# An S5 layer with GLU and ConvFFN: odd input tiles turned on TensorE, scanned states by GpSimd's queue, low halves of the GLU weights on VectorE

## The chip, the cores and the metric

One core of one Trainium2 chip runs the whole program. The metric is the device time of one execution in microseconds (us). The engines are called TensorE (PE), VectorE (DVE), ScalarE (ACT), GpSimd (POOL) and SyncE (SP); SyncE computes nothing here and only issues transfers. Each engine works through its own instructions in order; a transfer (DMA) is issued on the queue of one engine, SP, ACT or POOL.

## The reference

One layer with 2048 frames of 1024 channels, behind 16 learned meta tokens that are dropped at the end:

```python
h = jnp.concatenate([meta, x], axis=1)
hn = rms_norm(h, norm_mix[layer])
y = s5_mixer(hn, ...)           # below
h = h + y
hn = rms_norm(h, norm_ffn[layer])
h = h + conv_ffn(hn, ...)       # (silu(a) * b) @ w_down, a and b from a causal 3-tap conv of hn @ w_up
return h[:, N_META:]
```

The mixer is a linear recurrence with complex diagonal states in 64 groups of 16 channels, followed by a gated linear unit (GLU):

```python
u = (xn @ w_in).reshape(bsz, L, S5_GROUPS, S5_GROUP)
bu = einsum('gph,blgh->blgp', bb, u)              # complex input of the states
s = associative_scan(a * s_before + bu)           # 64 complex states a group
y = einsum(c_re, s_re) - einsum(c_im, s_im) + d_skip * u
y = gelu(y)
a, g = split(y @ w_glu, 2)
return a * sigmoid(g)
```

## The kernel before, in words

**Tiling.** Channels lie in eight blocks of 128 (`cb` or `p`, 0 to 7), frames in 16 tiles of 128, of which tile `r` takes every sixteenth frame; the meta tokens are a small 17th tile. Matrix products are made in f16 with three products: a value is held as a high half and a low half (`hi`, `lo`: the value minus its f16 rounding), and high × high, high × low and low × high are summed in fp32 (`mm3`, lines L76, L77, L78; in the GLU line L137).

**Head, to about 139 us.** For each x tile, `norm_a` (ACT squares, POOL makes 1/rms) and `norm_b` (L177 ACT high half, L178 DVE low half, L180 two transposing transfers on SP's queue, one for each half) put the normalised tile, turned so that channels are on the partitions, into `hnT`. The input weights come in column blocks; `split_win` scales them and makes their halves (ACT L354, L355, DVE L357 and others). `emit_u` makes u for a block and a quad of four tiles (512 columns), in parts as the tiles come; `evict_u` (POOL copies one column L404, ACT the rest L405) brings it from PSUM to `us`, and a transfer on SP to DRAM (`ud`), from where `load_u` fetches it as `U` in the order of the recurrence. Blocks 0, 1 and 2 are made in the head. In between `params` makes the recurrence's coefficients in small steps. An order written out by hand (a plan for each tile) sets what is emitted when.

**Periods p = 0 to 6, to about 408 us.** For block p: `gen_b`, `gen_c` on DVE (tables), `emit_v` on PE (the states' inputs), `scan(p)` on DVE (lines L547, L550, L552, in place in `S`), `emit_k` and `load_toep` (the Toeplitz matrix within 16 frames), `emit_z` (four transfers from the scanned `S` to `Z`, line L575), and one period later `emit_y(p-1)` on PE: products with Toep (L598, L599) and with Z (L600), gelu on ACT (L602) into `yf`, stored to `yd` by POOL (L606). PE fills up with the u of blocks 3 to 7 (`uq`). The last scan, p = 7, stands behind the loop.

**GLU weights.** `split_wg(i)` loads one of 16 slabs of 128 × 1024 on POOL's queue (L96) into a staging buffer `gst`, and makes its halves `wg`: a slab's high half by ACT in two steps (L102, L103) and its low half by POOL (L104), or both by DVE (L99, L100). Slab i belongs to depth `dk` = i // 2 of the product. Slabs 0 to 7 go by ACT and POOL in period 6 and beside the last scan, slabs 8 to 15 by DVE behind the last scan. `load_y` and `prep_y` fetch y from `yd` as `yt`, make its halves `yh` and turn them into `yT`; `glu_mm(t, d0, d1)` makes the products of tile t for depths d0 to d1.

**GLU loop (to about 739 us) and FFN.** 16 tiles of the GLU with the FFN's preparation, and then the FFN. The change does not touch them.

## Time and profile before

| | |
|---|---|
| median of 3 runs | 2039.63 us (2032.14 to 2040.07) |
| profiled execution | 2040.73 us, of which the span of the profile is 2038.9 us |
| granted TensorE clock, mean | 0.979 |
| busy over the span | PE 94%, DVE 68%, ACT 32%, POOL 28% |
| of this up to 739 us | the head, the scans and the GLU, where the change lies |

Rows of the profile are read like this: a group of instructions has its line, engine, operation, output <- inputs, the shape, the count, then busy time, mean ns of one, and the idle time in front of it with what ended it. A row of the timeline begins with start and length in us. A row by stage has the stretch, its length, the busy time of each engine with the count of instructions, the mean granted clock, the share of time for which the transfer engines were busy, and GB/s.

### The profile page before, as it was taken

Reading aid. Unit: us, or ns where it says so; the run is one execution under the profiler, and the core shown is the slowest. Engines: PE = TensorE matmul, PEld = TensorE weight load, DVE = VectorE, ACT = ScalarE, POOL = GpSimd, SP = SyncE. Lnnn points to the kernel's source line nnn. Section 1 sums busy time; section 2 is a strip of 40 time slices with the busy share of each in tenths; the row PEclk is TensorE's granted clock in tenths of the full one; section 3 lists DMA queues with packets and bytes.
Section 4 is the critical chain, followed back from the end, with each engine's and each line's share of the span. In section 5 each row is a group of like instructions: output and inputs, shape, how many; then the busy total and the mean of one; then the engine's idle time right before and its main releaser. Section 6 shows DMA issues by size and latency. Waiting matters only on the chain.

```text
span 2038.9 us, 28973 instructions
## 1 busy us (share of the span) xinstructions
PE 1923.3 (94%) x10992; PEld 957.5 (47%) x10992; DVE 1384.9 (68%) x1709; ACT 645.2 (32%) x1057; POOL 577.2 (28%) x644
## 2 busy tenths in 40 slices
PE   3699999689999999999999989999999999999999
PEld 3456666445444444444444434334444444444444
DVE  3489999944444348999999961345466666668982
ACT  5433423312222224544445441222222232322110
POOL 4221212400000014555555500366000001117630
PEclk9799999789999999999999999999999999999999
DMA  9967766958566656444444489999533333336443
GB/s 187 188 136 140 176 138 150 229 139 185 130 140 158 147 150 178 143 156 148 146 157 148 151 243 274 310 324 303 171 104 101 102 104 101 101 99 156 144 124 93
DMA packets 337223, 329.92 MB, mean 162 GB/s; under 512 B 150700, under 2 KB 238332, under 8 KB 337084
## 3 DMA queue, kind: packets, MB, share of 16 engines
q1 hardware_dynamic: 319164, 286.01, 52.9%
q0 software_dynamic: 8496, 27.30, 4.7%
q10 hardware_dynamic: 9424, 14.76, 2.9%
q8 instruction: 86, 1.41, 0.3%
q14 instruction: 53, 0.43, 0.1%
HBM read 183.82 MB, written 108.45 MB: 143 GB/s over the span
## 4 chain that ended last, share of the span: by engine, by line
PE 66%; DVE 8%; DMA 4%; issue 2%; ACT 1%; POOL 1%; SPq 1%; DVEq 0%; ACTq 0%; POOLq 0%
PE g L137 15%; PE p L78 11%; PE p L76 11%; PE p L77 11%; PE pq L76 3%; PE pq L77 3%; PE pq L78 3%; PE po L76 2%; PE po L77 2%; PE po L78 2%; DMA wc<-wcd 1%; DMA wcd<-wc 1%; DVE wc L914 1%; DVE y L1132 1%; DVE y L1131 1%
## 5 line engine op out<-in xcount | busy, mean ns | idle before, releaser
L76 PE MATMUL p<-hc,wc 128*128 128x512 f16 x1232 | 467.3, 379 | 2.3 <-DMA hc<-hl 1.7
L78 PE MATMUL p<-hc,wc 128*128 128x512 f16 x1232 | 467.5, 379 | 1.7 <-DVE wc L914 1.7
L77 PE MATMUL p<-hc,wc 128*128 128x512 f16 x1232 | 467.4, 379 | 0.9 <-DMA hc<-hl 0.9
L137 PE MATMUL g<-wg,yT 128*128 128x512 f16 x1536 | 334.3, 381 | 0.7 <-DMA yT<-yh 0.7
L914 DVE SCALAR_TENSOR_TENSOR wc<-fst,wc 128x512 f16<-128x512 f32 x209 | 184.7, 892 | 109.9 <-ACT wc L908 91.4
L137 PEld LDWEIGHTS <-yT 128*128 128x128 f16 x1536 | 150.2, 98 | 183.1 <-issue 2.6
L908 ACT ACTIVATE wc<-fst 128x512 f16<-128x512 f32 x209 | 125.9, 625 | 229.6 <-POOL fst L873 97.5
L78 PEld LDWEIGHTS <-wc 128*128 128x128 f16 x1232 | 120.2, 98 | 148.7 <-DVE wc L914 3.8
L76 PEld LDWEIGHTS <-wc 128*128 128x128 f16 x1232 | 120.1, 98 | 140.0 <-issue 1.8
L77 PEld LDWEIGHTS <-wc 128*128 128x128 f16 x1232 | 120.2, 98 | 138.9 <-DMA hc<-hl 1.2
L76 PE MATMUL pq<-wc,act 128*128 128x512 f16 x352 | 135.2, 384 | 16.6 <-DMA wc<-wcd 11.1
L76 PE MATMUL u<-hnT,win 128*128 128x512 f16 (+2 forms) x352 | 115.2, 337 | 25.6 <-DMA hnT<-hl 14.8
L77 PE MATMUL pq<-wc,act 128*128 128x512 f16 x352 | 135.1, 384 | 0.0
L78 PE MATMUL pq<-wc,act 128*128 128x512 f16 x352 | 134.8, 383 | 0.0
L77 PE MATMUL u<-hnT,win 128*128 128x512 f16 (+2 forms) x352 | 114.9, 337 | 16.9 <-DMA hnT<-hl 16.9
L76 PE MATMUL po<-wc,act 128*128 128x512 f16 x308 | 117.6, 382 | 3.4 <-DVE res L1292 3.4
L77 PE MATMUL po<-wc,act 128*128 128x512 f16 x308 | 117.6, 382 | 0.0
L78 PE MATMUL po<-wc,act 128*128 128x512 f16 x308 | 117.4, 381 | 0.0
L78 PE MATMUL u<-hnT,win 128*128 128x512 f16 (+2 forms) x352 | 115.0, 337 | 0.0
L1123 ACT ACTIVATE act<-hu,cwt 128x1024 f32<-128x1024 f32 x44 | 54.6, 1241 | 185.6 <-DVE hu L1224 141.3
L77 PEld LDWEIGHTS <-act 128*128 128x128 f16 x660 | 64.8, 98 | 99.1 <-issue 23.3
L1123 ACT ACTIVATE y<-hu,cwt 128x1024 f32<-128x1024 f32 x44 | 54.6, 1240 | 162.3 <-DVE hu L1224 123.2
(328 smaller groups left out, 2983.6 us busy)
## 6 DMA issues: line engine op xcount, KB each, us to landing
wc<-wcd SPq DMA_DIRECT2D x275, 256.0 KB, 2.7
wcd<-wc SPq DMA_DIRECT2D x253, 256.0 KB, 3.2
fst<-in_ffn_w_up_dram SPq DMA_DIRECT2D x44, 512.0 KB, 5.1
fst<-in_ffn_w_down_dram SPq DMA_DIRECT2D x44, 512.0 KB, 5.8
ud<-us SPq DMA_DIRECT2D x32, 258.0 KB, 5.3
U<-ud SPq DMA_DIRECT2D x16, 516.0 KB, 3.5
Toep<-kd SPq DMA_DIRECT2D x64, 128.0 KB, 5.4
yd<-yf POOLq DMA_DIRECT2D x8, 1024.0 KB, 7.6
```

Of the source, the lines that this page charges most:

```text
L76: PE.matmul(out=ps, lhsT=sh, rhs=mh, start=first, stop=False)
L77: PE.matmul(out=ps, lhsT=sh, rhs=ml, start=False, stop=False)
L78: PE.matmul(out=ps, lhsT=sl, rhs=mh, start=False, stop=last)
L137: PE.matmul(out=gps[t][o], lhsT=yT[t][:, a, dk], rhs=wg[b][:, dk, 512 * o:512 * o + 512], start=(dk == 0 and a + b == 0), stop=(dk == DK - ...
L908: A.activation(w[:, 0], src, AF.Copy, scale=GS)
L914: V.scalar_tensor_tensor(w[:, 1], src, GS, w[:, 0], op0=ALU.mult, op1=ALU.subtract)
L1123: A.activation(y, hu[:, 2:18], AF.Identity, bias=cwt[:, 3, c:c + 1], scale=cwt[:, 2, c:c + 1])
L1131: V.scalar_tensor_tensor(y, hu[:, 1:17], cwt[:, 1, c:c + 1], y, op0=ALU.mult, op1=ALU.add)
L1132: V.scalar_tensor_tensor(y, hu[:, 0:16], cwt[:, 0, c:c + 1], y, op0=ALU.mult, op1=ALU.add)
```

## The change

There are three parts.

*Head.* Odd tiles are no longer turned by transfers. `norm_t` scales the identity by 1/rms (DVE) and multiplies the x tile, in fp32, with it: eight products of 128 columns on PE, which turn and normalise at once; `norm_c` takes them out of PSUM as high half (ACT) and low half (DVE). Even tiles and the meta tile stay with `norm_b`. u is emitted by pairs of tiles (256 columns) for blocks 0, 1 and 2; the last quad of blocks 1 and 2 comes whole, behind that of block 0. The order is written anew: x loads six tiles ahead on ACT's queue, loads of the first tables in front of the transposes on SP, the split of the fourth weight block behind the last evictions; the small copy of `evict_u` moves from POOL to ACT.

*Queues.* `emit_z` issues on POOL's queue instead of SP's; the last block's `yd` store goes to SP; in period 6, `transp` and three slab loads are issued in front of Z.

*GLU weights.* ACT makes all 16 high halves, DVE all 16 low halves (by one subtraction from the scaled slab, L101), POOL none. There are nine staging slots. The first nine low halves stand directly behind the last scan, in front of what y's last block needs from DVE; products with high halves of depths 0 to 3 are emitted ahead of them, those with low halves behind them and in front of `emit_y(7)`; high halves 9 to 15 stand between and behind the gelus of `emit_y(7)`.

```diff
     def split_wg(i, pool, tag, bufs):
...
-        if wg_eng[0] is V:
-            V.tensor_scalar(wg[0][:, dk, cs_], st, GS, None, op0=ALU.mult)
-            V.scalar_tensor_tensor(wg[1][:, dk, cs_], st, GS, wg[0][:, dk, cs_], op0=ALU.mult, op1=ALU.subtract)
-        else:
-            A.activation(st, st, AF.Copy, scale=GS)
-            A.copy(wg[0][:, dk, cs_], st)
-            PO.tensor_tensor(wg[1][:, dk, cs_], st, wg[0][:, dk, cs_], op=ALU.subtract)
+        A.activation(st, st, AF.Copy, scale=GS)
+        A.copy(wg[0][:, dk, cs_], st)
+        yield
+        V.tensor_tensor(wg[1][:, dk, cs_], st, wg[0][:, dk, cs_], op=ALU.subtract)
+        yield
...
+        def norm_t(r, xt, rs):
+            dg = ld.tile([P, P], F32, tag="dg", bufs=1, name=f"dg{r}")
+            V.tensor_scalar(dg, ident, rs, None, op0=ALU.mult)
+            turned[r] = []
+            for h in range(2):
+                pt = psum.tile([P, 4, P], F32, tag="v", name=f"xT{r}_{h}")
+                for i in range(4):
+                    c = P * (4 * h + i)
+                    PE.matmul(out=pt[:, i], lhsT=xt[:, c:c + P], rhs=dg, start=True, stop=True)
+                turned[r].append(pt)
+
+        def norm_c(r):
+            for h, pt in enumerate(turned.pop(r)):
+                hi, lo = (t[:, 4 * h:4 * h + 4, r] for t in hnT)
+                A.copy(hi, pt)
+                V.tensor_tensor(lo, pt, hi, op=ALU.subtract)
...
-            PO.tensor_copy(us[:, :, 0:1], um[cb][:, 4 * q:4 * q + 4].unsqueeze(2))
+            A.copy(us[:, :, 0:1], um[cb][:, 4 * q:4 * q + 4].unsqueeze(2))
...
             for c in range(2):
                 for e in range(2):
-                    SY.dma_start(out=z.rearrange("p (q e) k -> p e q k", e=2)[64 * c:64 * c + 64, e],
+                    PO.dma_start(out=z.rearrange("p (q e) k -> p e q k", e=2)[64 * c:64 * c + 64, e],
                                  in_=S[cb][64 * e:64 * e + 64, :, c])
...
         for i, r in enumerate(seq):
...
+            if i + 2 < len(seq):
+                r2 = seq[i + 2]
+                (norm_t if r2 % 2 else norm_b)(r2, xt.pop(r2), na.pop(r2))
+            if i + 1 < len(seq) and seq[i + 1] in turned:
+                norm_c(seq[i + 1])
...
+            elif r % 2:
+                if r % 4 == 1 and r > 1:
+                    evicts(r // 4 - 1)
+                if r < T - 3:
+                    part_u(r // 4, r % 4 - 1)
                 else:
-                    evict_u(int(e[1]), int(e[2]))
+                    emit_u(0, 3, part=r - T + 3, w=2, tag=3)
...
-        wg_split(3, 4)
-        wg_load(7)
-        wg_load(8)
+        his, los = ((0, 0), (1, 0)), ((0, 1),)
+        wg_hi(3, 6)
         drive(gen_c(p))
-        glu_mm(0, 0, 1)
+        for i in range(6, 9):
+            wg_load(i)
+        glu_mm(0, 0, 2, his)
         emit_k(p)
         load_toep(p)
-        wg_split(4, 6)
         drive(scan(p))
-        emit_y(p - 1, lambda gp: wg_split(6 + gp, 7 + gp - gp // 2))
-        emit_z(p)
-        glu_mm(0, 1, 3)
+        emit_y(p - 1)
+        wg_hi(6, 8)
+        glu_mm(0, 2, 4, his)
         load_y(1, s5_tile, 0, NY[1])
         load_y(0, s5_tile, NY[0], NY[1])
-        wg_split(8, 12, V)
-        emit_y(p)
-        glu_mm(0, 3, NY[0])
-        prep_y(1, s5_tile, 0, NY[1], V)
-        prep_y(0, s5_tile, NY[0], NY[1], V)
-        wg_split(12, 16, V)
+        emit_z(p)
+        wg_lo(0, 9)
+        wg_hi(8, 9)
+        glu_mm(0, 0, 4, los)
...
+        emit_y(p, between)
+        wg_lo(9, 11)
+        glu_mm(0, 4, NY[0])
+        for i in range(11, 16):
+            wg_hi(i, i + 1)
+            wg_lo(i, i + 1)
```

PE at the start of the head, before: the first products of u (`win` is the weights, `hnT` the turned tiles, `tg` the norms' gains).

```order
L200 MATMUL tg<-ident,gst 128x16
L76 LDWEIGHTS win_163
L76 MATMUL u_0_195<-hnT_92,win_163 128x128
L77 LDWEIGHTS win_163
L77 MATMUL u_0_195<-hnT_93,win_163 128x128
```

The same place now: `xT` is the odd tile in PSUM, `dg` the scaled identity, `xt` the tile as loaded.

```order
L219 MATMUL tg<-ident,gst 128x16
L183 MATMUL xT_0_203<-dg_201,xt_136 128x128 x4
L183 MATMUL xT_1_208<-dg_201,xt_136 128x128 x4
L76 LDWEIGHTS win_172
L76 MATMUL u_0_267<-hnT_92,win_172 128x256
L77 LDWEIGHTS win_172
```

The eight products that turn tile 1 stand in front of the first product of u, which is 256 columns wide instead of 128.

VectorE behind the last scan, before (`S` the states, `stab7d` the scan's scratch):

```order
L552 TENSOR_TENSOR S_3710<-S_3710,stab7d_3859 128x8x63
L99 TENSOR_SCALAR wg_3489<-gst_0_3754 128x1024
L100 SCALAR_TENSOR_TENSOR wg_3490<-gst_0_3754,wg_3489 128x1024
L99 TENSOR_SCALAR wg_3489<-gst_1_3816 128x1024
L100 SCALAR_TENSOR_TENSOR wg_3490<-gst_1_3816,wg_3489 128x1024
```

And now:

```order
L571 TENSOR_TENSOR S_3755<-S_3755,stab7d_3901 128x8x63
L101 TENSOR_TENSOR wg_3538<-gst_0_3539,wg_3537 128x1024
L101 TENSOR_TENSOR wg_3538<-gst_1_3541,wg_3537 128x1024
L101 TENSOR_TENSOR wg_3538<-gst_0_3543,wg_3537 128x1024
L101 TENSOR_TENSOR wg_3538<-gst_1_3744,wg_3537 128x1024
L101 TENSOR_TENSOR wg_3538<-gst_0_3746,wg_3537 128x1024
L101 TENSOR_TENSOR wg_3538<-gst_1_3748,wg_3537 128x1024
L101 TENSOR_TENSOR wg_3538<-gst_0_3807,wg_3537 128x1024
L101 TENSOR_TENSOR wg_3538<-gst_1_3809,wg_3537 128x1024
L101 TENSOR_TENSOR wg_3538<-gst_0_3811,wg_3537 128x1024
L124 SCALAR_TENSOR_TENSOR yh_5_1_4059<-yt_5_3981,yh_5_0_4058 128x256
```

Nine low halves, from slab 0 on, stand where the high and low halves of slabs 8 to 11 stood.

GpSimd around the last scan, before:

```order
L104 TENSOR_TENSOR wg_3490<-gst_1_3531,wg_3489 128x1024
L96 DMA gst_0_3750<-in_s_w_glu_dram 128x1024
L96 DMA gst_1_3752<-in_s_w_glu_dram 128x1024
L96 DMA gst_0_3754<-in_s_w_glu_dram 128x1024
L104 TENSOR_TENSOR wg_3490<-gst_0_3544,wg_3489 128x1024
L96 DMA gst_1_3816<-in_s_w_glu_dram 128x1024
L104 TENSOR_TENSOR wg_3490<-gst_1_3557,wg_3489 128x1024
```

And now:

```order
L96 DMA gst_1_3748<-in_s_w_glu_dram 128x1024
L594 DMA Z_3750<-S_3446 64x4x128 x4
L96 DMA gst_0_3807<-in_s_w_glu_dram 128x1024
L96 DMA gst_1_3809<-in_s_w_glu_dram 128x1024
L96 DMA gst_0_3811<-in_s_w_glu_dram 128x1024
L625 DMA yd<-yf_3925 128x16x128
L594 DMA Z_3983<-S_3755 64x4x128 x4
```

Only transfers are left there, the states' among them.

More of the change, by code (lines that the diff above doesn't have):

```diff
@@ new lines, in tile_kernel, with part_u, evicts @@
+        drive(split_win(0, ws.pop(0)))
+        for r in seq[1:3]:
+            na[r] = norm_a(r, xt[r])
+        norm_t(1, xt.pop(1), na.pop(1))
+        splits = [split_win(cb, ws.pop(cb)) for cb in (1, 2)]
+        for g in splits:
+            next(g)
+        for r in (4, 5):
+            xt[r] = load_x(r, A)
+        def part_u(q, p):
+            for cb in range(3):
+                emit_u(cb, q, part=p, w=2, tag=cb if q == 0 else (3, 0, 1)[cb])
+        def evicts(q):
+            for cb in range(3):
+                evict_u(cb, q)
@@ new lines, in tile_kernel @@
+        for i, r in enumerate(seq):
+            if i + 6 < T:
+                xt[i + 6] = load_x(i + 6, A)
+            if i + 3 < len(seq):
+                r3 = seq[i + 3]
+                na[r3] = norm_a(r3, xt[r3])
+            if i + 2 < len(seq):
[3 more added lines that the diff above has]
+                norm_c(seq[i + 1])
+            if i < 2:
+                drive(splits[i])
+            for _ in range(1 if i == 0 else 2 if 3 <= i < 15 else 0):
+                next(par, 0)
+            if r == T:
@@ L760, in tile_kernel @@
             load_toep(p)
-            emit_z(p)
-            transp(p + 1)
+            if pen:
+                transp(p + 1)
+                for i in range(3, 6):
+                    wg_load(i)
+                emit_z(p)
+            else:
+                emit_z(p)
+                transp(p + 1)
             uq(2, range(0, 4))
```

116 lines of the change are left out of this document (49 added, 67 removed).

## The prediction, made before the changed kernel had run

> **What bounds the kernel now.** I read the busy time by stage first, cut where the work changes (head, periods, last two periods, GLU loop):
>
> ```profile
> 20.00:58.00 38.00, 22.62 (x348) 21.82 (x348) 13.67 (x21) 17.26 (x21) 19.30 (x24) 0.96 1.10 156
> 58.00:95.00 37.00, 21.35 (x160) 16.58 (x159) 12.94 (x39) 17.08 (x30) 10.49 (x22) 0.81 1.05 198
> 95.00:119.00 24.00, 23.45 (x96) 9.90 (x97) 20.59 (x37) 4.59 (x6) 3.65 (x6) 0.87 0.75 145
> ...
> 139.00:343.00 204.00, 198.16 (x1684) 128.56 (x1682) 199.49 (x281) 67.85 (x142) 42.47 (x70) 0.99 0.68 150
> 343.00:408.00 65.00, 44.39 (x378) 33.53 (x378) 63.09 (x73) 26.01 (x38) 26.07 (x21) 0.82 0.87 208
> ...
> 459.00:739.00 280.00, 279.72 (x1514) 130.09 (x1515) 118.97 (x148) 70.08 (x101) 19.56 (x43) 0.99 0.64 148
> ```
>
> Columns are window, length, then busy PE, PEld, DVE, ACT, POOL, granted clock, DMA share, GB/s. From 459 us on PE is full, so whatever is won or lost before it moves the end by as much. Until 95 us no engine is full but the DMA share is 1.05 to 1.10: the head waits for transfers. From 139 to 343 PE (198.2 of 204) and DVE (199.5) are both full. From 343 to 408 DVE alone is (63.1 of 65), PE has 20 us of room.
>
> Then the head's rows: SyncE's issues (length is what the queue spent), the transposes' landing, the first quad's end, one cold and one warm product of 256 columns, the fp32 products of 128 columns, and the point where the u of block 0 is complete.
>
> ```profile
> 103.59 6.61 SPq L180 DMA_TRANSPOSE hnT<-hl  x4
> hnT<-hl SPq DMA_TRANSPOSE x32, 8.5
> 55.95 0.17 PE L76 MATMUL um<-hmT,win 128*128 128x16 f16 x1
> 61.68 0.39 PE L77 MATMUL u<-hnT,win 128*128 128x256 f16 x1 [1.93 <-DMA hnT<-hl]
> 61.87 0.42 PE L78 MATMUL u<-hnT,win 128*128 128x256 f16 x1
> 67.44 0.27 PE L78 MATMUL u<-hnT,win 128*128 128x256 f16 x1
> 67.55 0.27 PE L76 MATMUL u<-hnT,win 128*128 128x256 f16 x1
> 121.00:126.00 5.00, 5.00 (x24) 1.08 (x3) 1.00 1.01 172
> L465 PE MATMUL wt<-ident,wit 128*128 128x128 f32 x16 | 2.2, 280 | 0.2 <-ACT Win L467 0.2
> 120.02 2.06 ACT L405 ACTIVATE us<-u 128x512 f32<-128x512 f32 x4
> 138.94 0.30 DVE L700 TENSOR_SCALAR cwt<-tcv 128x132 f32<-128x132 f32 x1 [3.83 <-PE tcv L699]
> ```
>
> 32 transposes leave SyncE at 1.65 us (6.61/4) each at the quickest and land 8.5 us later; u of block 0 is ready at 119.5, and DVE's saturated run begins at 138.94.
>
> **Term 1, the head.** 16 of the 32 transposes go. At 1.65 us that is 26 us of transfers or more, so the DMA stops being the bound and PE's own work sets the pace. A pair of tiles now costs PE 3 blocks × 8 × 3 = 72 products of 256 columns at 0.11 us (67.44 to 67.55) = 7.9 us, and 8 fp32 products that turn the odd tile, at 2.2/16 = 0.14 us, 1.1 us: 9.0 us. I keep 56 us as the end of the first quad (the row at 55.95), although fewer transposes may bring it forward. Behind it stand four pairs (36 us) and, for block 0 alone, two pairs of 24 + 8 products (2 × 3.7 us): 99.5 us with no gap. Each odd tile's chain (square, rstd, scaled identity, products, two casts, two subtractions) runs one pair ahead, and ACT issues the x loads later; I allow a gap of about 1 us a pair and take 105 us for u of block 0, against 119.5. What follows (u of blocks 1 and 2 for the last quad, at the same 24 products in 5 us, the load of U, the first states) is the same 19.5 us; the third weight split now lies behind it, about 1 us. Gain 13 us. Bounds: no gap and an earlier first quad, 18; the pace of before (63.5 us for the same quads) in spite of it all, 0. I take 13, nearer to the products' rows than to a pace set by transfers that are no longer there.
>
> **Term 2, the last two periods.** GpSimd subtracts eight GLU slabs here, and each subtraction lies on a stretched VectorE instruction:
>
> ```profile
> 386.12 2.33 POOL L104 TENSOR_TENSOR wg<-gst,wg 128x1024 f16<-128x1024 f32 x1 [10.42 <-ACT wg L103]
> 389.32 2.13 POOL L104 TENSOR_TENSOR wg<-gst,wg 128x1024 f16<-128x1024 f32 x1
> L104 POOL TENSOR_TENSOR wg<-gst,wg 128x1024 f16<-128x1024 f32 x8 | 17.7, 2213 | 28.6 <-ACT wg L103 28.6
> 385.89 0.63 DVE L550 TENSOR_TENSOR S<-S,stab7u 128x256 f32<-128x256 f32 x1
> 386.56 2.37 DVE L552 TENSOR_TENSOR S<-S,stab7u 128x256 f32<-128x256 f32 x1
> 388.96 2.91 DVE L547 TENSOR_TENSOR stab7u<-S,asc 128x256 f32<-128x256 f32 x1
> 392.76 0.59 DVE L547 TENSOR_TENSOR stab7k<-S,asc 128x240 f32<-128x240 f32 x1
> ```
>
> Of one size, with and without a subtraction beside it: 2.37 against 0.63 (+1.74), 2.91 against 0.59 (+2.32). The mean, 2.03, times eight is 16.3; the smaller times eight 13.9; the subtractions' whole time 17.7. The chain of waits goes through VectorE's scan to its last instruction (407.69, below), and VectorE has 1.9 us without work in these 65, so all of it is on the path. Now no tensor instruction is left on GpSimd here. VectorE gains 16.3 us, and PE, with 44.4 us of work and 32 − 12 = 20 GLU products (20 × 0.21 = 4.2 us) more, has 65 − 16.3 = 48.7 us for 48.6: just enough, since the last of it may run over the scan's end. Bounds 12 (PE 4 us late with it) and 17.7; I take 16.3.
>
> **Term 3, the tail,** counted from the last scan's end (408.4):
>
> ```profile
> 407.69 0.70 DVE S L552
> ...
> 410.47 5.41 DMA Z<-S
> 415.93 1.22 PE yp L600 x2
> 424.54 30.88 PE g L137 x143
> 455.69 3.19 DMA yT<-yh
> 458.92 21.11 PE g L137 x97
> L100 DVE SCALAR_TENSOR_TENSOR wg<-gst,wg 128x1024 f16<-128x1024 f32 x8 | 9.8, 1225 | 0.3
> L102 ACT ACTIVATE gst<-gst 128x1024 f32<-128x1024 f32 x8 | 8.4, 1052 | 0.0
> L103 ACT CAST wg<-gst 128x1024 f16<-128x1024 f32 x8 | 8.4, 1046 | 0.3
> ```
>
> Before, y of the last block starts when Z lands, at +7.5 us (415.93), and ends at +16.1 (424.54). The first two GLU tiles have 2 × 96 products, 36 of them ahead of this y; the 156 behind it take 33.7 us at 30.88/143 each, to +49.8, just before the third tile's start at 458.92 (+50.5). Now 16 products with low halves stand ahead of this y on PE, and the last of them needs the eighth low half: 8 × 1.23 = 9.8 us, so they end at about +10.7, and y at +19.3: 3.2 us later. 48 products are done by then and 144 are left, 2.6 us less. Then ACT, which now makes every high half, needs 1.05 + 1.05 = 2.1 us a slab, and slabs 11 to 15 come behind the last gelu and slab 10, at +24 to +33, their low halves 1.2 us later. PE wants a dk (two slabs) every 2.6 us and gets one every 4.2: I count waits of 1, 3 and 2 us for the low halves of slabs 9, 11 and 13, and none for 15, since the second tile's products stand ahead. Loss 3.2 − 2.6 + 6 = 6.6, say 7 us. Bounds: 2 (PE seldom waits) and 12 (the five slabs' 10.5 us in the open, and the 3.2 us of yT at 455.69 behind them).
>
> **Term 4, states by GpSimd's queue.** The rows are eight Toeplitz loads and four loads of scanned states on SyncE's queue, PE's wait for these, and transfers of the same kind of pieces on either queue:
>
> ```profile
> 330.34 6.22 SPq L522 DMA_DIRECT2D Toep<-kd  x8
> 336.68 7.56 SPq L575 DMA_DIRECT2D Z<-S  x4
> 345.93 0.43 PE L588 MATMUL mp<-U,Toep 128*32 128x1 f32 x32 [3.25 <-DMA Z<-S]
> 190.31 0.70 POOL L422 DMA_DIRECT2D X<-in_s_b_re_dram  x1
> X<-in_s_b_re_dram SPq DMA_DIRECT2D x2, 32.0 KB, 3.2
> X<-in_s_b_re_dram POOLq DMA_DIRECT2D x2, 32.0 KB, 3.2
> ```
>
> At 336.68 Z came out of SyncE's queue behind the Toeplitz loads and PE waited 3.25 us; on GpSimd's queue nothing stands in front of it but loads and a store whose data are there. An issue costs 0.70 us there in the midst of the scans, and the transfer lands after 3.2 us from either queue. So 0 on the sum: the 3.3 us are PE's, and DVE is the bound there. Bounds: +3, and a loss that is the third rival. The Trainium skill speaks against this edit: "SBUF — State Buffer", section "SBUF: two separate sides", says that GpSimd writes the descriptors of its queue's transfers through the ports that it shares with VectorE, so that such a transfer stands still while VectorE holds them (about 620 ns becoming about 3100). The row at 190.31 does not show it, for the instructions that ran beside it; by that page four issues could take some 12 us, and the sum would be the third rival's.
>
> **The sum.** 13 + 16.3 − 7 + 0 = 22.3 us off the profiled execution of 2040.7 us: 2018.4. The median of the runs is 2039.6, 1.1 us lower: **2017 us**. With the terms' bounds taken half way each: 2008 to 2027. A measurement of this kernel tells about 0.5% from no change: 10 us, so faster means below 2029.
>
> **The rivals.**
>
> First, PE sets the head at a low clock. After a wait the products are 0.42 us long and 0.2 us apart (61.68 and 61.87) where they are else 0.27 and 0.11, up to some 5.5 us later (67.44 is quick again). Half speed for 5.5 us loses 2.7 us, and the granted clock between 58 and 95 us was 0.81. If every pair begins so and waits 2 us for its tile, a pair costs 9.0 + 2.7 + 2 = 13.7 us, u of block 0 comes at 56 + 4 × 13.7 + 7.4 = 118, the head gains 1, and with a tail at its dear end (−10) the sum is 1 + 16.3 − 10 = 7.3: 2032, no change. "TensorE: Matmul & The Clock Gate", Part 1, of the Trainium skill has this as its rule (half the clock after about 3.4 us idle, until the array has been busy as long); the row at 61.68 follows a wait of only 1.93 us, so the trace has it easier to fall into than the page. Against it: gaps of that length came from transposes, and half of them are gone.
>
> Second, the stretch is not GpSimd's doing (the page's spans on POOL are rough), or it returns through the eight subtractions that VectorE now has: 13 − 7 = 6, 2033, no change. Against it: eight of eight coincide, and the low halves stand behind the scan, where they are already in the tail's term.
>
> Third, slower: GpSimd's queue is held up while VectorE works without a pause (199.5 of 204 us), with weight splits among its instructions:
>
> ```profile
> L357 DVE TENSOR_TENSOR win<-wst,win 128x1024 f16<-128x1024 f32 x3 | 5.7, 1895 | 5.6 <-ACT win L355 5.6
> ```
>
> If each of the four issues waits out an instruction of 1.2 us (L100 above) to 1.9 us (the weight splits' row, here), Z lands some 6 us (4 × 1.5) late in each of the six periods. PE has 204 − 198.2 = 5.8 us of idle time in all of them, so 36 − 5.8 = 30 us go to PE and from there to the scans, whose inputs PE makes; with the last Z (+6, hidden in part by the wait for low halves, 3) the sum is 22.3 − 30 − 3 = −10.7: 2050. It decides from about 4 us of lateness a period. Against it the two rows of X and the issue of 0.70.
>
> Fourth, all of it works: head 18, last periods 17.7, tail −2: 2006.
>
> **How the numbers follow.** My sum 0.60; head at a low clock 0.17; stretch stays 0.04; slower 0.09; all works 0.10. Predicted time 2017. Faster: 0.60 + 0.10 and a part of the first rival, 0.74; slower 0.09; within 0.5%: 0.17. The range of 8 in 10 leaves out the slow rival and half of the fast one: 2004 to 2036.
>
> **What would show it.** Head: no transposes of odd tiles, u of block 0's eviction near 105 us instead of 120, PE busy over 80% from 58 us on at a clock above 0.9. Last periods: no VectorE instruction of the scan over 1.3 us, the scan's end near 379 (408.4 − 13 − 16.3). Tail: PE's wait in front of y named after low halves, then waits for wg in the first GLU tile, and the third GLU tile near +57 instead of +50.5. Queue: Z from GpSimd landing in under 5 us. I am wrong if Z is what PE waits for in the periods, if u of block 0 is not before 115, or if the GLU begins more than 12 us later behind the scan than before.

## The result, and the profile after

The change made the kernel slower. The median of 19 runs is 2048.38 us (2039.16 to 2055.0), beside 2033.48 us (2026.43 to 2042.19) of 19 runs of the kernel before: a ratio of 1.0062 with a 95% interval of 1.005 to 1.0075, some 12.6 us more by that ratio, where 22.3 us less were forecast.

The two profiled executions hide part of this. That of before (2040.73 us) lies 7 us above its median, that of after (2046.09 us) 2 us below. So I compare by stage, and hold every stage against several executions, since each experiment keeps parts of the old kernel.

By stage (windows of the kernel after; the columns are those of the prediction's first fence, which has the rows of before):

```profile
20.00:58.00 38.00, 17.35 (x122) 14.88 (x123) 13.54 (x17) 15.18 (x24) 14.12 (x18) 0.69 0.81 167
58.00:95.00 37.00, 37.00 (x395) 33.89 (x393) 21.37 (x68) 21.09 (x44) 16.75 (x27) 1.00 0.67 151
95.00:119.00 24.00, 23.43 (x195) 18.95 (x194) 17.29 (x45) 5.51 (x14) 4.61 (x7) 1.00 0.43 103
139.00:343.00 204.00, 194.25 (x1669) 127.12 (x1662) 193.14 (x271) 70.14 (x160) 47.46 (x72) 0.98 0.68 147
343.00:408.00 65.00, 41.46 (x312) 29.35 (x311) 57.48 (x82) 28.44 (x38) 13.35 (x22) 0.84 0.78 183
408.00:425.00 17.00, 12.21 (x93) 9.16 (x92) 1.43 (x3) 3.08 (x7) 2.10 (x4) 1.00 0.89 285
```

From 58 us on the head is now PE's (37.00 of 37 busy at clock 1.00, 21.35 at 0.81 before), but its first 38 us are poorer than before (17.35 at 0.69, against 22.62 at 0.96). From 139 to 343 PE was busy for 3.9 us less than before and DVE for 6.4 us less, and since the periods' work is the same, they waited for more. From 343 on no engine is full: PE 41.46 of 65, DVE 57.48, and behind the scan the transfers have the highest share (0.89).

**The head** (timeline of the kernel after; SP, PE, DVE and ACT together):

```profile
10.41 0.74 SPq L441 DMA_DIRECT2D X<-in_s_b_re_dram  x1
17.60 3.10 SPq L199 DMA_TRANSPOSE hnT<-hl  x2
35.12 0.40 PE L77 MATMUL u<-hnT,win 128*128 128x256 f16 x1 [10.82 <-DMA hnT<-hl]
46.97 0.15 DVE L225 MEMSET zero<- 128x112 f32 x1 [8.52 <-PE xT L183]
52.78 0.29 DVE L177 TENSOR_SCALAR dg<-ident,rsa 128x128 f32<-128x128 f32 x1 [2.97 <-DMA kd<-zero]
53.17 3.11 PE L183 MATMUL xT<-dg,xs 128*128 128x128 f32 x13 [5.90 <-issue]
64.43 0.17 PE L76 MATMUL um<-hmT,win 128*128 128x16 f16 x1
66.25 0.80 PE L183 MATMUL xT<-dg,xs 128*128 128x128 f32 x5
75.97 1.95 PE L183 MATMUL xT<-dg,xs 128*128 128x128 f32 x16
114.05 0.61 ACT L424 ACTIVATE us<-u 128x512 f32<-128x512 f32 x1
132.88 0.30 DVE L726 TENSOR_SCALAR cwt<-tcv 128x132 f32<-128x132 f32 x1
```

The first transposes now stand behind the table loads in SP's queue (10.41, 17.60), and the first low-half product of u comes at 35.12 (33.78 before), at half speed: 0.40 us, and 0.42 each for those behind it, against 0.27 in the prediction's row at 67.44. The scaled identity `dg` has one slot, and `zero`, which `zero_kd` stores to `kd`, now uses the same: the fill of `zero` waits 8.52 us for the products that read `dg` (46.97), the next `dg` waits for the store (52.78), and PE stands for 5.90 us (53.17). A steady pair then takes 75.97 − 66.25 = 9.7 us. u of block 0 is complete with the eviction at 114.05. (A turn has 16 records, two for each product; the rows with 13 and 5 are parts of one.)

**The periods** (timeline of the kernel after, POOL and DVE, at period 1, and what the tile view of X names as ending DVE's idle time, in us and times):

```profile
196.15 2.48 POOL L594 DMA_DIRECT2D Z<-S  x4 [15.93 <-issue]
198.62 0.71 POOL L441 DMA_DIRECT2D X<-in_s_b_re_dram  x1
207.06 0.69 DVE L454 TENSOR_TENSOR tx<-X,coef 128x512 f32<-128x512 f32 x1 [2.39 <-DMA X<-in_s_b_re_dram]
```
```profile
  DMA X<-in_s_b_re_dram: 7.2, 4
```

Z is issued as the scan ends, and only behind it come the loads of the tables X for the next period. Before, X was issued at 190.31 (the prediction's row), while that scan ended at 200.91. DVE, which never waited for X there, now waits four times, 7.2 us in all: 2.39, 1.42 and 0.56 within the five periods from scan 0 to scan 5, and 2.88 behind scan 5.

**The last two periods and the tail.** The same tile group in the two traces, of three scan steps of one size each, first before, then after:

```profile
L547 DVE TENSOR_TENSOR stab7u<-S,asc 128x1024 f32<-128x1024 f32 (+2 forms) x3 | 5.2, 1739 | 0.1
```
```profile
L566 DVE TENSOR_TENSOR stab7u<-S,asc 128x1024 f32<-128x1024 f32 (+2 forms) x3 | 2.9, 962 | 0.1
```

The scan is quick now. But y of block 6 is not earlier (timeline; before, then after):

```profile
360.68 2.73 SPq L515 DMA_DIRECT2D kd<-ks  x4
369.86 5.51 SPq L522 DMA_DIRECT2D Toep<-kd  x8
384.65 0.61 PE L588 MATMUL mp<-U,Toep 128*32 128x1 f32 x32 [1.30 <-DMA Toep<-kd]
```
```profile
362.42 4.26 SPq L534 DMA_DIRECT2D kd<-ks  x4
373.31 6.21 SPq L541 DMA_DIRECT2D Toep<-kd  x8
388.55 0.61 PE L607 MATMUL mp<-U,Toep 128*32 128x1 f32 x32 [10.77 <-DMA kd<-ks]
394.38 0.69 DVE L571 TENSOR_TENSOR S<-S,stab7d 128x504 f32<-128x504 f32 x1
401.14 1.05 ACT L98 ACTIVATE gst<-gst 128x1024 f32<-128x1024 f32 x1
401.53 1.18 POOL L625 DMA_DIRECT2D yd<-yf  x1 [22.35 <-ACT yf L621]
402.70 0.65 POOL L594 DMA_DIRECT2D Z<-S  x1
407.36 1.23 DVE L101 TENSOR_TENSOR wg<-gst,wg 128x1024 f16<-128x1024 f32 x1 [0.81 <-ACT wg L99]
418.65 0.42 ACT L121 ACTIVATE yh<-yt 128x256 f16<-128x256 f32 x1 [5.02 <-DMA yt<-yd]
427.10 7.70 PE L135 MATMUL g<-wg,yT 128*128 128x512 f16 x24 [4.63 <-ACT wg L99]
462.46 0.82 PE L135 MATMUL g<-wg,yT 128*128 128x512 f16 x3 [0.71 <-DMA yT<-yh]
```

The Toeplitz matrix of block 6 goes by SP to DRAM and back: store at 362.42, loads from 373.31, products at 388.55: 26 us, where it took 24 before (360.68 to 384.65), and no engine's busy time shows it. PE waits 10.77 us for it. (The profile puts the end of this wait down to a later store, `kd`, that was under way then; the products read the matrix, and before, in e10 and in e11 the same wait is put down to its load.) The last scan ends at 394.38 + 0.69 = 395.07, 13.3 us earlier than before, and finds y of block 6 (`y(6)` below) still under way; the high halves of slabs 6 to 8 (ACT, from 401.14) stand behind its gelus, the last of the first low halves (407.36) behind these, and Z of block 7, whose states are done at 395.07, behind the store of y in POOL's queue (402.70). ACT, whose order has the first preparation of y between two gelus of block 7, then stands 5.02 us for y's load (418.65), which could only leave behind that store. The third GLU tile begins at 462.46, 67.4 us behind the scan, not 50.5.

The milestones of every kernel below are read from its trace like this, one profiled execution each. "Scan 0" is the end of the first scan's last instruction of 504 elements; the others count from the same point of scan 5.

| kernel | scan 0 | scan 0 to 5 | scan 7 | y(6) begins | y(7) ends | third GLU tile |
|---|---|---|---|---|---|---|
| before | 167.0 | 165.9 | 75.4 | 51.7 | 91.6 | 126.0 |
| after | 161.0 | 171.4 | 62.6 | 56.1 | 89.6 | 130.0 |
| e1 head alone | 158.3 | 166.0 | 75.8 | 50.5 | 93.0 | 127.4 |
| e2 states alone | 154.2 | 166.2 | 79.6 | 57.1 | 97.5 | 131.9 |
| e3 GLU weights alone | 156.6 | 166.0 | 60.7 | 58.5 | 92.6 | 133.0 |
| e4 tables first | 159.7 | 166.6 | 68.9 | 67.7 | 101.2 | 141.9 |
| e5 head, own slot | 152.9 | 166.0 | 75.9 | 50.7 | 93.0 | 127.3 |
| e6 Toeplitz early | 152.8 | 166.1 | 58.4 | 60.3 | 91.5 | 132.5 |
| e7 order behind scan | 151.9 | 166.0 | 63.5 | 59.5 | 94.6 | 133.8 |
| e8 both | 162.1 | 166.0 | 58.4 | 63.6 | 93.3 | 132.9 |
| e9 states' own slot | 156.4 | 166.0 | 64.7 | 59.4 | 95.2 | 133.8 |
| e10 matrix first | 159.8 | 166.1 | 58.5 | 49.1 | 88.6 | 127.1 |
| e11 e10 + mended head | 155.5 | 166.0 | 58.5 | 56.5 | 94.6 | 133.7 |
| e12 e11 + queue | 154.4 | 166.2 | 59.3 | 60.0 | 95.2 | 135.3 |
| e13 no late loads | 154.5 | 166.2 | 58.5 | 54.6 | 81.8 | 121.3 |
| e14 loads later | 153.6 | 165.9 | 58.5 | 51.4 | 79.2 | 126.3 |
| e15 e14 + mended head | 156.5 | 166.0 | 58.6 | 49.9 | 81.6 | 128.6 |

From the third GLU tile to the end of the span it is 1580.0 us before and 1581.8 after: the loss lies ahead of it.

### The profile page after: what moved, and what is told of

The parts are those of the page before. It is cut to its first block, busy times and chain, and to the rows that moved or that the text cites. A ratio compares the mean times of both kernels' runs of the same rounds, so it can differ in the third digit from the quotient of the medians.

```text
span 2044.3 us, 29075 instructions
## 1 busy us (share of the span) xinstructions
PE 1935.3 (95%) x11072; PEld 975.7 (48%) x11072; DVE 1371.2 (67%) x1722; ACT 667.5 (33%) x1116; POOL 563.6 (28%) x635
## 4 chain that ended last, share of the span: by engine, by line
PE 78%; DMA 8%; DVE 5%; issue 4%; ACT 3%; POOL 2%; SPq 1%; ACTq 0%; DVEq 0%; POOLq 0%
PE g L135 14%; PE p L76 12%; PE p L77 12%; PE p L78 12%; PE pq L76 3%; PE pq L77 3%; PE pq L78 3%; PE po L76 2%; PE po L77 2%; PE po L78 2%; PE u L76 2%; PE u L78 2%; PE u L77 2%; DMA Z<-S 1%; DMA wcd<-wc 1%
## 5 line engine op out<-in xcount | busy, mean ns | idle before, releaser
L135 PE MATMUL g<-wg,yT 128*128 128x512 f16 x1536 | 339.0, 383 | 13.6 <-ACT wg L99 8.0
L957 ACT ACTIVATE wc<-fst 128x512 f16<-128x512 f32 x209 | 125.9, 625 | 227.3 <-POOL fst L922 97.5
L77 PE MATMUL u<-hnT,win 128*128 128x512 f16 (+1 forms) x336 | 111.4, 331 | 10.8 <-DMA hnT<-hl 10.8
L76 PE MATMUL u<-hnT,win 128*128 128x512 f16 (+1 forms) x336 | 111.5, 332 | 5.9 <-DMA hnT<-hl 4.9
L1172 ACT ACTIVATE act<-hu,cwt 128x1024 f32<-128x1024 f32 x44 | 54.6, 1241 | 186.1 <-DVE hu L1273 144.4
L78 PE MATMUL u<-hnT,win 128*128 128x512 f16 (+1 forms) x336 | 111.4, 331 | 1.3 <-DVE win L376 1.3
L1172 ACT ACTIVATE y<-hu,cwt 128x1024 f32<-128x1024 f32 x44 | 54.6, 1241 | 162.3 <-DVE hu L1273 123.1
```

Source lines behind the costliest of these rows:

```text
L76: PE.matmul(out=ps, lhsT=sh, rhs=mh, start=first, stop=False)
L77: PE.matmul(out=ps, lhsT=sh, rhs=ml, start=False, stop=False)
L78: PE.matmul(out=ps, lhsT=sl, rhs=mh, start=False, stop=last)
L135: PE.matmul(out=gps[t][o], lhsT=yT[t][:, a, dk], rhs=wg[b][:, dk, 512 * o:512 * o + 512], start=(dk == 0 and a + b == 0), stop=(dk == DK - ...
L957: A.activation(w[:, 0], src, AF.Copy, scale=GS)
L1172: A.activation(y, hu[:, 2:18], AF.Identity, bias=cwt[:, 3, c:c + 1], scale=cwt[:, 2, c:c + 1])
```

## The experiments

Where an expectation has theories, A is the one held when it was written and B (or C) a rival. Ratios are against the kernel before on the same chip, with 95% intervals.

### The parts alone

**e1**, the head of the change in the kernel before; Z stays on SP, the GLU weights as before:

```diff
+            zero = ld.tile([P, 7 * T], F32, tag="dg", bufs=1, name="zero")
+            (norm_t if r2 % 2 else norm_b)(r2, xt.pop(r2), na.pop(r2))
```

> The kernel before with the new head alone (odd tiles turned on PE, the new order of loads and splits); scanned states by SyncE's queue and the GLU weights as before. From the trace of the changed kernel the head is worth 6 us (end of the first scan 160.98 against 167.04). Theory A, the head keeps what it wins: 6 us faster than before, 0.997, and all scans' ends 6 us earlier. Theory B, the head's gain is of no use because VectorE and PE then wait for something else in the periods: equal to before by the last scan. If the idle time before the third tile's fp32 products (5.9 us) comes from the scaled identity sharing a slot with the zeros that are being stored, it stands here at the same place.

Measured: 2033.11 us against 2028.97, 1.0024 [1.0009, 1.0038]. The new head by itself is slower by 4.9 us; PE's idle 5.91 us in front of tile 5's products is there again. Neither theory had the head slower than the old one.

**e2**, Z of blocks 0 to 5 on POOL's queue, nothing else:

```diff
-                    SY.dma_start(out=z.rearrange("p (q e) k -> p e q k", e=2)[64 * c:64 * c + 64, e],
+                    (PO if cb < 6 else SY).dma_start(out=z.rearrange("p (q e) k -> p e q k", e=2)[64 * c:64 * c + 64, e],
```

> The kernel before with one line changed: scanned states of blocks 0 to 5 loaded by GpSimd's queue, those of 6 and 7 by SyncE's as before. Theory A, the loads of the tables X stand behind the scanned states in GpSimd's queue and so wait for the end of the scan, and VectorE waits for X in the next block: VectorE has waits for X of 1 to 3 us in four or five periods (none before), the last scan ends 5 to 8 us later, ratio 1.003. Theory B, GpSimd's queue is slow under a busy VectorE: the states land some 6 us late, PE waits for them and VectorE does not wait for X. Theory C, neither: 0.

Measured: 2035.36 against 2028.97, 1.0023 [1.0011, 1.0035]: 4.7 us slower. In its timeline (SP's last transposes, ACT, DVE):

```profile
91.43 6.59 SPq L180 DMA_TRANSPOSE hnT<-hl  x4
108.38 2.06 ACT L405 ACTIVATE us<-u 128x512 f32<-128x512 f32 x4
126.13 0.29 DVE L700 TENSOR_SCALAR cwt<-tcv 128x132 f32<-128x132 f32 x1 [2.64 <-PE tcv L699]
334.43 0.69 DVE L435 TENSOR_TENSOR tx<-X,coef 128x512 f32<-128x512 f32 x1 [4.90 <-DMA X<-in_s_b_re_dram]
```

The wait for X is there with this edit alone, 4.90 us at the last table and 0.22 at one other: the mechanism holds, with two waits where after has four. But the long one lies behind scan 5: the five periods take 166.2 us as before, and it is the last scan that ends 4.2 us later (79.6 for 75.4). The first three rows show something else: with the old head the last transposes left at 91.43, u of block 0 was complete at 108.38 and the saturated run began at 126.13, not at 103.59, 120.02 and 138.94.

**e3**, only the GLU weights' part, with Z of blocks 6 and 7 on POOL as the change has it:

```diff
-            PO.tensor_tensor(wg[1][:, dk, cs_], st, wg[0][:, dk, cs_], op=ALU.subtract)
+        V.tensor_tensor(wg[1][:, dk, cs_], st, wg[0][:, dk, cs_], op=ALU.subtract)
```

> The kernel before with the GLU part alone (all high halves on ScalarE, all low halves on VectorE, none on GpSimd; scanned states of blocks 6 and 7 by GpSimd's queue, those of 0 to 5 by SyncE's; the head as before). From the trace of the changed kernel: the last two scans shorter by some 13 to 16 us, and the third GLU tile starts 66 to 68 us behind the last scan's end instead of 50.5. Theory A, what the scans win is lost behind them, because ScalarE and y of block 6 are late: sum +1 to +4 us, 1.001. Theory B, the tail is late in the changed kernel only because the head and the queue disturb it: 8 us faster or more.

Measured: 2039.77 against 2028.97, 1.0051 [1.0037, 1.0066], 10.4 us slower, although the last scan ends 14.7 us earlier behind scan 5 (60.7 for 75.4). y(6) begins 6.8 us later, y(7) ends 1.0 us later, the third tile begins 7.0 us later. All three parts lose; the sum of their losses (0.98%) is more than the whole change's (0.62%), so they overlap.

### Undoing one cause at a time

**e4**, the kernel after with the loads of X in front of Z on POOL's queue:

```diff
+                bcn = load_bc(p + 2)
                 emit_z(p)
                 transp(p + 1)
...
-            if p + 2 < NCB:
-                bcn = load_bc(p + 2)
```

> The changed kernel with the tables' loads for block p+2 issued by GpSimd in front of the scanned states of block p instead of behind them; nothing else. Theory A (tables held behind the states): VectorE's waits for X (2.39, 1.42, 0.56 and 2.88 us in the changed kernel) go, the last scan ends 5 to 7 us earlier than in the changed kernel (395.1), time 5 to 7 us under it. Theory B (the queue itself is slow): PE's waits for the states stay at 7 us, the scans' ends stay within 1 us.

Measured: 2048.56 against 2028.97, 1.0096 [1.0083, 1.0109]: not faster than the change. The waits for X are gone and the first five periods are back at 166.6 us. But then (DVE and PE, kernel e4):

```profile
357.99 0.83 DVE L124 SCALAR_TENSOR_TENSOR yh<-yt,yh 128x640 f16<-128x640 f32 x1 [10.63 <-ACT yh L121]
394.03 0.60 PE L607 MATMUL mp<-U,Toep 128*32 128x1 f32 x32 [13.37 <-DMA kd<-ks]
```

So A is right about the waits and wrong about the time: what was won in the periods is lost at the low half of y and at y(6), which begins 67.7 us behind scan 5.

**e5**, e1 with `zero` in a slot of its own:

```diff
-            zero = ld.tile([P, 7 * T], F32, tag="dg", bufs=1, name="zero")
+            zero = s5.tile([P, 7 * T], F32, tag="bb", bufs=2, name="zero")
```

> The kernel before with the new head alone, and the zeros that are stored to the Toeplitz buffer in a slot of their own instead of the scaled identity's. With the shared slot PE stands idle for 5.91 us before the fp32 products of tile 5, and the scaled identity is made at 49.91, behind the store. Theory A (the shared slot): this idle time goes, u of block 0 comes 5 us earlier, the first scan ends near 153 instead of 158.3, ratio 0.9995 instead of 1.0024. Theory B (the x tile or its 1/rms is late anyway): the idle time stays over 4 us and the ratio at 1.002.

Measured: 2026.21 against 2029.36, 0.9995 [0.9982, 1.0007]. In its timeline (DVE, PE, ACT):

```profile
44.69 0.28 DVE L179 TENSOR_SCALAR dg<-ident,rsa 128x128 f32<-128x128 f32 x1
45.07 3.47 PE L185 MATMUL xT<-dg,xs 128*128 128x128 f32 x16 [1.58 <-issue]
106.03 0.61 ACT L426 ACTIVATE us<-u 128x512 f32<-128x512 f32 x1
124.85 0.28 DVE L728 TENSOR_SCALAR cwt<-tcv 128x132 f32<-128x132 f32 x1
```

The idle 5.91 us are 1.58, and the run begins at 124.85 where e1 had 130.21. So the shared slot costs the head what e1 lost. The mended head has u of block 0 at 106.03, close to the 105 that were forecast, but the old one has it at 108.38 in e2: the mended head is as quick as the old one, not quicker.

**e6**, e3 with the way of the Toeplitz matrix of block 6 freed on SP and PE (the transposes of y behind its loads, the first GLU products behind `emit_k`):

```diff
-            if pen:
-                fills.append(prep_y(0, s5_tile, 0, NY[0]) for _ in range(1))
...
             load_toep(p)
             if pen:
+                prep_y(0, s5_tile, 0, NY[0])
...
-        glu_mm(0, 0, 2, his)
         emit_k(p)
         load_toep(p)
+        glu_mm(0, 0, 2, his)
```

> The GLU part alone, with the preparation of y for the first GLU tile moved behind the Toeplitz loads of block 6, so that SyncE's transposes (3.0 us) no longer stand in front of the stores and loads that give the Toeplitz matrix. Theory A (y of block 6 waits for this matrix, and everything behind it follows): the loads go out 3 to 5 us earlier, y of block 6 begins earlier by as much (381.1 in the run without this edit, 23 us behind the scan before), and the third GLU tile too; time 3 to 5 us under the GLU part alone. Theory B (only ScalarE's high halves set the tail): y earlier, the third tile within 1 us of where it was.

Measured: 2037.76 against 2029.36, 1.0030 [1.0001, 1.0059]. Inconclusive on the matrix: the GLU products, still in front of y(6) on PE, now waited 13.18 us for the late transposes, and y(6) began at 60.3.

**e7**, e3 with another order behind the scan: Z(7) on SP right behind it, nine high halves in front of it, the low halves' products behind y(7), y's halves last:

```diff
+        wg_hi(6, 9)
         drive(scan(p))
+        emit_z(p)
         emit_y(p - 1)
-        wg_hi(6, 8)
...
         emit_y(p, between)
-        wg_lo(9, 11)
+        wg_lo(9, 12)
+        glu_mm(0, 0, 4, los)
         glu_mm(0, 4, NY[0])
```

> The GLU part alone, with another order in the tail: high halves 6 to 8 in front of the gelus of block 6; the last scanned states by SyncE as soon as the scan ends; the products with low halves of depths 0 to 3 behind y of block 7 instead of in front of it; high halves 9 to 11 between the gelus of block 7 and the preparation of y behind them. Theory A (the order makes the tail): third GLU tile 58 to 62 us behind the last scan's end instead of 72.3, time 10 to 14 us under the GLU part alone (ratio 0.999 or less instead of 1.0051). Theory B (ScalarE has too much to do with 16 slabs of 2.1 us, in any order): 70 us or more, ratio within 0.001 of 1.005.

Measured: 2036.19 against 2029.36, 1.0034 [1.0014, 1.0054]. No better behind scan 5 (133.8): Z has one slot, which y(6) reads till its end, so Z(7) could not leave before 389.66, 8 us behind the scan. The store of y(6) went to SP here too.

**e8**, both, e6's edit on e7:

```diff
-            if pen:
-                fills.append(prep_y(0, s5_tile, 0, NY[0]) for _ in range(1))
...
+        glu_mm(0, 0, 2, his)
         wg_hi(6, 9)
```

> The edits of the two runs above together on the GLU part alone. If both theories A hold, they add: y of block 6 earlier by 3 to 5 us and the third tile 52 to 58 us behind the scan; 14 to 18 us under the GLU part alone, ratio 0.996 to 0.998. If the Toeplitz matrix is not in the way once the order is mended: as the order alone.

Measured: 2038.36 against 2029.36, 1.0037 [1.002, 1.0053]; y(6) began at 63.6.

**e9**, e7 with a slot of its own for Z(7), and eight staging slots instead of nine:

```diff
-            z = s5.tile([P, G, P], F32, tag="Z", name=f"Z{cb}")
+            z = s5.tile([P, G, P], F32, tag="Z" if cb < NCB - 1 else "pim", name=f"Z{cb}")
```

> The kernel of e7 (GLU part alone, other order behind the scan), with the last scanned states in a slot of their own, so that their load need not wait until y of block 6 has read the states before; for it one staging slot is given up (eight slabs instead of nine). In e7 the load was issued at 389.66, 8 us behind the scan's end, as y of block 6 ended, and PE waited 6.96 us for it. Theory A (the states' slot holds y of block 7): the load goes out within 1 us of the scan's end, y of block 7 ends 7 to 8 us earlier and the third GLU tile comes 5 to 7 us earlier, 126 to 128 us behind the scan of block 5 instead of 133.8. Theory B (the Toeplitz matrix of block 7 is the next wait): half of it or less.

Measured: 2036.75 against 2030.39, 1.0030 [1.0012, 1.0048]. Z(7) left with the scan's end, and had no use of it (its DMA issues from 375 to 430 us):

```profile
gst<-in_s_w_glu_dram POOLq DMA_DIRECT2D x8, 512.0 KB, 10.0
Z<-S SPq DMA_DIRECT2D x4, 128.0 KB, 12.0
```

Beside eight slab loads a transfer of the states, 5.41 us before (the prediction's row at 410.47), needs 12.0 us. The kernel before makes these loads too, but most of them one after another as its subtractions free the slots: ten from 357 us to the end of its last scan and three behind it (410.53 to 414.26). Here the low halves free eight slots within 8 us, at the time of Z(7).

**e10**, e9 with all of tile 0's high-half products behind y(6), and the transposes of y behind the Toeplitz loads (e6's edit without its fault):

```diff
-        glu_mm(0, 0, 2, his)
         emit_k(p)
         load_toep(p)
...
         emit_y(p - 1)
-        glu_mm(0, 2, 4, his)
+        glu_mm(0, 0, 4, his)
```

> The kernel of e9, with the preparation of y for the first GLU tile behind the Toeplitz loads of block 6 (as in e6), and all products with high halves of depths 0 to 3 behind y of block 6 (in e6 they stood in front of it and themselves waited for the transposes). Theory A (y of block 6 waits for the way of the Toeplitz matrix through DRAM): y of block 6 begins 28 to 31 us behind the products that make it (35 in e7), the third GLU tile comes 117 to 122 us behind the scan of block 5 (before: 126 to 127), and the kernel is 4 to 8 us faster than before, 0.997. Theory B (transfers are the bound there, whatever the order): 126 or more, equal to before or slower.

Measured: 2036.8 against 2030.39, 1.0022 [1.0003, 1.0041]. y(6) begins at 49.1, y(7) ends at 88.6, the third tile at 127.1: 6.7 us better than e9 in the trace, and yet no gain over before, as B had it.

**e11** is e10 with the mended head of e5 (its edit stands there), **e12** e11 with Z of all blocks but the last on POOL and X in front of it: the change as a whole, mended where causes had been found.

```diff
-                    (PO if cb == 6 else SY).dma_start(out=z.rearrange("p (q e) k -> p e q k", e=2)[64 * c:64 * c + 64, e],
+                    (PO if cb < 7 else SY).dma_start(out=z.rearrange("p (q e) k -> p e q k", e=2)[64 * c:64 * c + 64, e],
...
+                bcn = load_bc(p + 2)
                 emit_z(p)
```

> The kernel of e10 with the new head, the zeros in a slot of their own (as in e5). The head with its own slot was as fast as the old one (0.9995). If the parts add: as e10, within 2 us. If the head's shorter transfers at the end of the head help the periods: 2 to 4 us faster than e10.

> The kernel of e11 with the scanned states of blocks 0 to 5 by GpSimd's queue as well, the tables' loads in front of them (as in e4): all three parts of the change, each mended. If the tables' place was all that was wrong with the queue, it equals e11 or wins up to 3 us (PE's waits for the states behind the Toeplitz loads in period 5); if the queue costs by itself, it is 3 us slower or more.

Measured: 2034.57, 1.0020 [1.0005, 1.0036], and 2039.76, 1.0031 [1.001, 1.0051], both against 2030.39. e11 has the code of e10 behind scan 5, and its third tile began at 133.7 instead of 127.1, though by their ratios the two kernels are level; the profiled execution of e11 is the slowest of its twelve (2041.29). So much can two executions differ there, and I draw nothing from single differences of that size. e12's median lies 5.2 us above e11's, while their intervals overlap: whether the queue costs something even with X in front stays open.

### The transfers behind the scan

**e13**, e10 without the loads of slabs 8 to 15. Their halves are made from the staged slabs 0 to 7 again, so the second half of the GLU's weights is not the reference's; all other work is done in full:

```diff
-        st = pool.tile([P, D], F32, tag=tag, bufs=bufs, name=f"gst{dk}_{hh}")
-        PO.dma_start(out=st, in_=w_glu[0, dk * P:(dk + 1) * P, cs_])
+        if i < 8:
+            st = gsts[i] = pool.tile([P, D], F32, tag=tag, bufs=bufs, name=f"gst{dk}_{hh}")
+            PO.dma_start(out=st, in_=w_glu[0, dk * P:(dk + 1) * P, cs_])
+        else:
+            st = gsts[i - 8]
```

> The kernel of e10 without the loads of GLU slabs 8 to 15 (4 MB): these slabs are made from the staging tiles of slabs 0 to 7, in the same order and with the same engine work, so that the GLU's second half of weights is not the reference's. Theory A (behind the scan the transfers are the bound: eight slab loads go out together with the last states and the store of y): the last states land within 5 us of their issue (up to 11.8 in e10), y of block 7 ends 78 to 82 us behind the scan of block 5 instead of 88.6, the third GLU tile at 114 to 119 instead of 127.1, time 8 to 12 us under e10. Theory B (the order of ScalarE's work): third tile within 3 us of e10's.

Measured: 2023.0 against 2031.45, 0.9953 [0.9933, 0.9972], the only kernel clearly below the one before. Of its DMA issues from 375 to 425 us, and of PE's waits:

```profile
Z<-S SPq DMA_DIRECT2D x4, 128.0 KB, 5.9
410.07 2.76 PE L138 MATMUL g<-wg,yT 128*128 128x512 f16 x12 [1.61 <-DMA yT<-yh]
```

Z lands in 5.9 us instead of 11.8 (e10), y(7) ends at 81.8, the third tile begins at 121.3. With all else of the GLU part as in e10, whose ratio is 1.0022, the eight loads are worth 0.7%, some 14 us; the two traces, one execution each, show 5.8 of them before the third tile (121.3 for 127.1), later than the 114 to 119 of A. The kernel before was not run without its late loads, so this prices the loads in e10's order and does not compare them with before's.

**e14**, e10 with slabs 10 to 15 loaded later, by SP, behind the store of y and its load; **e15**, e14 with the mended head:

```diff
-        PO.dma_start(out=st, in_=w_glu[0, dk * P:(dk + 1) * P, cs_])
+        (PO if i < 10 else SY).dma_start(out=st, in_=w_glu[0, dk * P:(dk + 1) * P, cs_])
...
         wg_lo(0, 8)
+        for i in range(10, 16):
+            wg_load(i)
```

> The kernel of e10 with slabs 10 to 15 loaded by SyncE's queue behind the store and load of y, instead of all eight at once as the low halves free their slots; high halves behind the gelus, but for one. Theory A (transfers collide): the third GLU tile at 118 to 122 us behind the scan of block 5, 5 to 8 us under e10, 0.997 to 0.999 of before. Theory B (the order of ScalarE's work): as e10 or later, because high halves 9 to 15 come later.

> The kernel of e14 with the new head, zeros in their own slot. If the parts add, as e14 less 0 to 1 us (the head with its own slot was 0.9995 of before).

Measured: 2032.35, 0.9995 [0.9977, 1.0014], and 2030.64, 1.0001 [0.9985, 1.0018], both against 2031.45: level with before. In e14 y(7) ends 79.2 us behind scan 5, 12 us earlier than before, and then PE waits (timeline of e14):

```profile
411.44 1.03 PE L135 MATMUL g<-wg,yT 128*128 128x512 f16 x2 [6.72 <-DMA yT<-yh]
414.52 25.79 PE L135 MATMUL g<-wg,yT 128*128 128x512 f16 x108 [2.05 <-ACT wg L99]
```

The third tile is at 126.3, as before and later than A's 118 to 122. In the medians, moving the loads gives back e10's loss, not e13's gain (the intervals of e10 and e14 overlap). No kernel that computes everything was clearly faster than the one before.

## Why the prediction was wrong

**Term 1, the head, +13: wrong, by a false base and two missed waits.** The mechanism was right: DMA left the bound and PE took it, at clock 1.00, with a pair at 9.7 us for the 9.0 forecast (the turn of a tile is 1.95 us, not 1.1: each of its eight products leaves two records, 16 of 0.12 us in all, where the price row, a transpose, has one record for each of its 16). Two steps failed. "I keep 56 us as the end of the first quad": the small products that mark it (55.95 before) begin at 64.43. In front of them are now two turns, products at half the clock (granted 0.69 up to 58 us, 0.96 before), a start 1.3 us later behind SP's table loads, and above all the 5.90 us in which PE waits for `dg`, because `zero` shares its slot. So u of block 0 came at 114.05 instead of 105. That slot is the settled cause (e1 against e5): without it the first quad ends at 56.4 and u comes at 106.03. And the base: I took before's 138.94 and 119.5 for the old head. With that same head u of block 0 came at 108.38 and the run began at 126.13 in e2, and scan 0 ended at 151.9 to 162.1 in the nine experiments that keep it, with 154.5 in the middle; the profiled 167.0 is the latest of ten. There was nearly nothing to win: half the transposes gone makes a head that is equal (e5, 0.9995), and e1 as written 4.9 us slower. The first rival, "PE sets the head at a low clock" (head +1), was nearer, though its low clock sits in the first 58 us and not at every pair. Its reading of the row at 61.68 does not hold either: the wait of 1.93 us there stands behind another (the kernel before, PE), with 0.65 us of products between the two, so the row does not show that a single wait of 1.93 us is enough.

```profile
59.10 0.17 PE L76 MATMUL um<-hmT,win 128*128 128x16 f16 x1 [1.57 <-issue]
```

**Term 2, the last two periods, +16.3: right.** The last scan, counted from scan 5, ends 14.7 us earlier with the GLU part alone (e3), 16.9 in e10 (75.4 − 58.5) and 12.8 in the change itself, which has a wait of 2.88 us for X there. The forecast 16.3, eight stretched instructions at a mean of 2.03 us, lies among these, and no scan step over 1.3 us is left. The Trainium skill says in "SBUF — State Buffer", section "SBUF: two separate sides", that GpSimd and VectorE take a shared port pair as an exclusive lock, with two SBUF inputs on VectorE against a GpSimd operation that reads SBUF; the trace agrees (1739 ns a step becoming 962). The second rival, that the stretch stays, falls.

**Term 3, the tail, −7: this step failed.** "From 343 to 408 DVE alone is" full was read as: what DVE gains, the end gains, and the tail was "counted from the last scan's end". But y(6) hangs on another chain of nearly the same length, the Toeplitz matrix's way through DRAM (a store, a load, 26 us in after). y(6) began 49 to 68 us behind scan 5 in all runs, whether the last scan ended 58 or 80 us behind it. So the scan's gain ended in waits: PE's 10.77 us for the matrix, and behind it those for Z(7) and y's load, which follow the store of y(6) and meet the slab loads. What I counted from the scan's end was therefore 8 us too early for y(7) (it ends at +27 instead of +19.3), and the third tile comes at +67.4 instead of +57: the sign "the GLU begins more than 12 us later behind the scan than before" is met, with 16.9. The part of the term on PE's waits for wg in the first GLU tile was right: 6 us forecast, 4.63 + 0.92 + 0.24 measured. e7 to e9 show that the order behind the scan alone does not bring the gain back, and e10 not clearly that the matrix does (1.0022 for e9's 1.0030). e13 shows that the loads hold it up: without half the slabs' loads, and nothing else changed from e10, the GLU part gains 0.47% over before instead of losing 0.22%, although its y(6) began 5.5 us later than e10's. That the bunching of the loads, and not their mere number, makes the difference to before is read from the traces (three behind before's scan, eight in e10) and from e14, and was not tried on the kernel before. The sum with the tail at its right size: e3 says −10.4 for Terms 2 and 3 together, where +9.3 was forecast.

**Term 4, the queue, 0: this step failed too.** "On GpSimd's queue nothing stands in front of it but loads and a store whose data are there" looked ahead of Z and not behind it. Behind it stand the loads of X, which had run during the scan and now wait for its end; DVE, the bound in the periods, waits for them (7.2 us in after, of which 4.4 in the five periods, which take 171.4 for 165.9; 4.9 behind scan 5 in e2, which is 4.7 us slower). e4 takes these waits away and the periods are back at 166.6, so that cause of the waits is shown; what they are worth is shown by e2 alone, since e4 lost the time again behind scan 5.

The third rival, Z late from GpSimd's queue, had 2050 us, the time nearest to the measured 2048, by luck: its way to it did not happen. For Z of blocks 0 to 5 PE waits 7.2 us in after and 6.0 before, so Z is hardly later from POOL. Its four issues take 2.48 us in the midst of DVE's work, 0.62 each, and the standstill that the prediction weighed by the Trainium skill ("SBUF — State Buffer", section "SBUF: two separate sides") is not seen in these rows. That section has it for a VectorE copy, and not for `tensor_tensor`, which the scan's instructions are; so the estimate of some 12 us for four issues did not apply here.

**The sum.** Against the old head's middle (scan 0 at 154.5) the stages add up: head 161.0 − 154.5 = 6.5, periods 171.4 − 165.9 = 5.5, from scan 5 to the third GLU tile 130.0 − 126.0 = 4, together 16, beside 14.9 between the medians and 12.6 by the ratio. Each is one execution and good to several us only.

**Open.** Why the same old head took up to 15 us longer in one execution than in another; why the way of the Toeplitz matrix varies as it does (y(6) at 49.1 and 56.5 with the same code); what exactly keeps e14 from e13's gain beside the two waits shown; whether GpSimd's queue costs something beside the place of X (e12 against e11); and why the three parts together lose less than their sum. That the table loads in front of the first transposes cost the head something was read from the trace only, and not tried alone.

## What to carry to other kernels

When the bounding engine is relieved, look for the second chain of the same length before counting the gain, above all one that goes through DRAM and back, since no engine's busy time shows it; then count the tail from the later of the two. When loads are freed by an engine that has become quick, ask what else wants the transfers in the same microseconds. When a waiting transfer is moved to another in-order queue, list what stands behind it there, and who needs that. And take the base of a forecast from several executions, since one profile can be the worst draw of the very stage to be improved.
